# The low part of split weights: from a VectorE subtraction to a ScalarE pass and an accumulating DMA, in a one-core hybrid layer kernel

## The chip, the core and the metric

The kernel runs on one core of a Trainium2 chip. The core has a matrix engine (PE in the profile; its weight loads are listed as PEld), a vector engine (DVE), an activation engine (ACT), a general engine (POOL, GpSimd) and an engine that issues DMAs (SP). Each works through its own queue of instructions in order and waits on semaphores; DMAs run beside them on 16 DMA engines. The metric is the device time of one execution in microseconds; less is better. Before the change three runs took 1127.03, 1127.97 and 1128.79 us; the median is 1127.97 us.

## The reference

One layer for 512 prompt tokens and 64 sample tokens, each of width 1024. Three branches are fed by one projection of the normed input (`w_in`, 1024 rows), merged with sigmoid gates, and projected once more:

```python
h = _rmsnorm(x, norm_pre_w)
proj = h @ w_in
glu_v, glu_g, conv_gate, z, xbc, dt_raw, q, xa_gate, gates = jnp.split(proj, points, axis=-1)
u = glu_v * jax.nn.sigmoid(glu_g)                      # A: gated convolution, width 31
c, new_a = _causal_dwconv(u, st_a, conv_dw_w, conv_dw_b)
c = jax.nn.silu(_layernorm(c, conv_ln_w, conv_ln_b)) * jax.nn.silu(conv_gate)
out_a = c @ conv_out_w
...
y, new_h = _ssd_scan(xh, dt, a, bm, cm, st_h)          # B: state-space scan, 32 heads
...
out_b = y @ ssd_out_w
...
o = softmax(q k^T / 16) v                              # C: attention to 256 memory tokens, 4 heads
out_c = (o * jax.nn.silu(xa_gate)) @ xa_out_w
m = g[:, :, 0] * out_a + g[:, :, 1] * out_b + g[:, :, 2] * out_c
x_new = x + _rmsnorm(m @ w_out, norm_post_w)
```

The memory keys and values are computed for the prompt (`xa_kv_w`). Also returned are the keys and values, the tails of the two convolutions and the final states of the scan. All is in float32.

## The kernel before

The prompt and sample tokens are treated as one block of T = 576 columns. Activations lie with channels on the partitions, so a projection multiplies a weight tile of 128 columns with the normed input.

**Split arithmetic.** A float32 product is made of three matmuls in a rounded 32-bit type (float32r). Each operand is split in a high part, which is the value rounded to that type, and a low part, which is the rest. `mac` (L198 to L208) issues, for each block of 128 rows, high x high, high x low and low x high, so the low part of a weight (`wlo`) is first read by the third pair of matmuls of a job. `hT[0]` and `hT[1]` are the two parts of the normed input.

**Weight jobs.** `order` (from L89) is a list of 153 jobs in the order in which they are used: 512 KB of weights each, but for the narrow `dt`, for which 128 KB are loaded. `prep_to(n)` (L165 to L191) works this list up to job n: it takes a `raw`, a `whi` and a `wlo` tile from a pool with three buffers of each, loads `raw` through SP's queue (L172), makes the high part on ACT (L182) and the low part on DVE (L183):

```python
a = nc.scalar.activation(hi[:, :n_], raw[:, :n_], AF.Copy)
b = nc.vector.tensor_tensor(lo[:, :n_], raw[:, :n_], hi[:, :n_].bitcast(F32), ALU.subtract)
```

`W(name)` (L193) is called when a projection begins; it prepares the weights two jobs ahead (`LA = 2`). `dt` has lines of its own (L179, L180). With three buffers, the high part of a job can be written as soon as PE has done with the job three places before it, and PE reads it when the two jobs between are done.

**Stages.** After the start (norm and transposes of x, to about 25 us of the trace) comes the scan with four groups of heads, 20 chunks in all (`chunk_a`, `chunk_b`), whose small matmuls stand between projections for z, B, C and x and the output projection of the group before. Then follow the gated convolution's inputs (`glu`, with `gg` and `gv` jobs), the gates `g1`, the attention stage (four heads; jobs `k`, `q`, `v`, `xg`, where a `k` or `v` job has 24 matmuls of 256 columns, and any other but `dt` has 48 of about 288), the rest of the gates and output projections (`g2`, `oc`, `cg`, `g0`, `oa`), and the last projection, which loads and splits `w_out` at its own lines (L1075, L1083, L1084). The 31 taps of the long convolution (L768) run on DVE in the background of the attention and gate stages.

**What sets the order.** The program is written in a language whose scheduler simulates the engines and puts each engine's instructions in an order of its own, except where a line asks to keep the program's. So a change to some instructions can also move others. Semaphores are put in by it.

**Queues that the change touches.** SP issues the weight loads, each when its `raw` buffer is free, and, in the same queue, the scan's loads R (L497) and E (L516) of decay rows from a scratch tensor and the stores. POOL has 170 short instructions: copies of convolution tails (L445, L446), preparation of the padded inputs (L441, L442, L726, L727) and of the long convolution's tails (`utail`, L730, L731), and it issues no DMA.

Of the kernel before, what the change touches and what calls it, by code (L numbers as in the profile page):

```python
# [8 lines left out]
F32 = mybir.dt.float32  # L9
F32R = mybir.dt.float32r  # L10
AF = mybir.ActivationFunctionType
ALU = mybir.AluOpType
# [16 lines left out]
def hybrid_trunk_kernel(  # L29
# [9 lines left out]
    nc = tc.nc  # L39
# [15 lines left out]
    def ps_tile():  # L55
        return pps.tile([128, 512], F32, tag="ps", name="ps")

    # ------------------------------------------------------------ constants
    ident = const.tile([128, 128], F32, name="ident")
    make_identity(nc, ident)  # L60
    onesr = const.tile([128, 128], F32R, name="onesr")
# [14 lines left out]
    tails = const.tile([128, 2, 3, 24], F32, name="tails")  # L76
# [8 lines left out]
    msc = dram.tile([8, 128, T], F32, name="msc")  # L85
    scr = dram.tile([5, 32, 128], F32, name="scr")

    # ------------------------------------------------------------ weights
    order = []  # L89

    def wjob(name, src, c0, r0=0, kk=8, cols=128):
# [71 lines left out]
    nprep = [0]  # L163

    def prep_to(n):  # L165
        while nprep[0] <= min(n, len(order) - 1):
            name, src, c0, r0, kk, cols = order[nprep[0]]
            raw = wp.tile([128, 1024], F32, tag="raw", name="raw", bufs=3)
            hi = wp.tile([128, 1024], F32R, tag="whi", name="whi", bufs=3)
            lo = wp.tile([128, 1024], F32R, tag="wlo", name="wlo", bufs=3) if name != "dt" else hi  # L170
            n_ = kk * cols
            nc.sync.dma_start(  # L172
                out=raw[:, :n_].rearrange("p (k c) -> p k c", k=kk),
                in_=src[r0:r0 + 128 * kk, c0:c0 + cols].rearrange("(k p) c -> p k c", p=128),
            )
            if name == "dt":
                w = hi[:, :2 * n_].rearrange("p (k c) -> p k c", k=kk)
                rw, wh, wl = raw[:, :n_].rearrange("p (k c) -> p k c", k=kk), w[:, :, 0:32], w[:, :, 32:64]
                a = nc.scalar.activation(wh, rw, AF.Copy)  # L179
                b = nc.vector.tensor_tensor(wl, rw, wh.bitcast(F32), ALU.subtract)  # L180
            else:
                a = nc.scalar.activation(hi[:, :n_], raw[:, :n_], AF.Copy)  # L182
                b = nc.vector.tensor_tensor(lo[:, :n_], raw[:, :n_], hi[:, :n_].bitcast(F32), ALU.subtract)  # L183
            if nprep[0] in (2, 3):
                tc.keep_in_program_order(a)
                tc.keep_in_program_order(b)
            ready[name] = (w, None) if name == "dt" else (
                hi[:, :n_].rearrange("p (k c) -> p k c", k=kk),
                lo[:, :n_].rearrange("p (k c) -> p k c", k=kk),
            )  # L190
            nprep[0] += 1  # L191

    def W(name):  # L193
        i = pos[name]
        prep_to(i + LA)
        return ready.pop(name)
# [26 lines left out]
    def v2(ap):  # L223
        return ap.rearrange("p (a b) -> p a b", a=2)

    # ------------------------------------------------------------ start: x, parameters
    st = ExitStack()
    s2 = st.enter_context(tc.tile_pool(name="s2", bufs=2, reuse_waits="tile"))
    hl = [st.enter_context(tc.tile_pool(name="hl4", bufs=4, reuse_waits="tile"))]
# [8 lines left out]
        out=mask, in_=mask, pattern=[[1, 128]], compare_op=ALU.is_ge, fill=0.0,  # L238
# [4 lines left out]
    for t in range(5):  # L243
        n = 128 if t < 4 else 64
        if t < 4:
            x_t = obf[:, D * t:D * t + D]
        else:
            x_t = s2.tile([128, D], F32, tag="M", name="x4")
        nc.sync.dma_start(out=x_t[:n], in_=xp_d[128 * t:128 * t + 128] if t < 4 else xs_d)
        xt.append((x_t, n))  # L250
        if t == 0:
            wpre = s2.tile([128, D], F32, tag="R", name="wpre")
            nc.sync.dma_start(out=wpre, in_=norm_pre_w[0].partition_broadcast(128))
        if t == 1:
            prep_to(1)
# [58 lines left out]
    def tr_act(tiles, k, dst, wcol, ncols):  # L314
# [18 lines left out]
        out=after, in_=after, pattern=[[-1, 128]], compare_op=ALU.is_ge, fill=0.0,  # L333
# [64 lines left out]
        nc.scalar.activation(acsT[:, 512:640], pt[:32, 1, 0:128], AF.Copy)  # L398
        nc.sync.dma_start(out=scr.rearrange("c h l -> h c l"), in_=acsT.rearrange("p (c l) -> p c l", c=5))

    # parameters in channel-major columns
    vraw = s2.tile([104, 128], F32, tag="cbm", name="vraw")
    for o, src, n in (
        (V_PRE, norm_pre_w, 8), (V_MEM, mem_norm_w, 8), (V_GB, gate_b, 24), (V_DWB, conv_dw_b, 8),
# [28 lines left out]
            load_t(dww, 124 * i, flat(conv_dw_w, 124 * i, 124), 124, 0.5)  # L433
            load_t(sta, 120 * i, flat(state_conv_a[0], 120 * i, 120), 120, 2.0)

    # ------------------------------------------------------------ SSD
    def conv4(name, jt, tag, bufs, pt=None):
        if pt is None:
            pt = proj(name, HB)
        xp = s2.tile([128, 582], F32, tag="xp", name="xp")  # L440
        nc.gpsimd.memset(xp[:, 0:3], 0.0)  # L441
        nc.gpsimd.tensor_copy(xp[:, 515:518], sts.rearrange("p (r j) -> p r j", r=3)[:, :, jt])  # L442
        nc.scalar.activation(v2(xp[:, 3:515]), pt[:, :, 0:256], AF.Copy)
        nc.scalar.activation(xp[:, 518:582], pt[:, 1, 256:320], AF.Copy)
        nc.gpsimd.tensor_copy(tails[:, 0, :, jt], xp[:, 512:515])  # L445
        nc.gpsimd.tensor_copy(tails[:, 1, :, jt], xp[:, 579:582])  # L446
        acc = s2.tile([128, 579], F32, tag="acc", name="acc")
        w4 = scw.rearrange("p (r j) -> p r j", r=4)
        nc.scalar.activation(  # L449
            acc, xp[:, 0:579], AF.Identity, scale=w4[:, 0, jt:jt + 1], bias=half[:, V_SCB + jt:V_SCB + jt + 1]  # L450
        )
        for r in range(1, 4):
            nc.vector.scalar_tensor_tensor(acc, xp[:, r:r + 579], w4[:, r, jt:jt + 1], acc, ALU.mult, ALU.add)  # L453
        nc.scalar.activation(xp[:, 0:579], acc, AF.Tanh)
        o = sx.tile([128, 640], F32, tag=tag, name=tag, bufs=bufs)
        nc.gpsimd.memset(o[:, T:640], 0.0)
        nc.vector.scalar_tensor_tensor(o[:, 0:512], xp[:, 0:512], 1.0, acc[:, 0:512], ALU.add, ALU.mult)
        nc.vector.scalar_tensor_tensor(o[:, 512:576], xp[:, 515:579], 1.0, acc[:, 515:579], ALU.add, ALU.mult)
        return o
# [335 lines left out]
    glu(4, sx, "xs", 7)  # L795
    push_conv(2, 3)

    # tails of the short convolution
    for s, dst in ((0, o_csp), (1, o_css)):
        p = ps_tile()  # L800
        nc.tensor.transpose(p[:72, :128], tails[:, s].rearrange("p r j -> p (r j)"), ident)
# [2 lines left out]
        for r in range(3):  # L804
            nc.sync.dma_start(
                out=dst[0, 0, r].rearrange("(j c) -> j c", c=128), in_=tb[24 * r:24 * r + 24]
# [144 lines left out]
            if h != 2:  # L951
                push_conv(3 + h, 4 + h)

    # tails of the long convolution
    for b in range(2):
        p = ps_tile()
        for j in range(4):
# [4 lines left out]
        nc.sync.dma_start(out=o_cas[0, 0, :, 512 * b:512 * b + 512], in_=tu[30:60])  # L962
    st3.close()

    # ------------------------------------------------------------ out_c
    st3 = ExitStack()
    e2 = st3.enter_context(tc.tile_pool(name="e2", bufs=2, reuse_waits="tile"))
    hlA = st3.enter_context(tc.tile_pool(name="hlA", bufs=8, reuse_waits="tile"))
# [54 lines left out]
    stx.close()  # L1023
    stx = ExitStack()

    # ------------------------------------------------------------ layer norm, conv gate
    hlB = stx.enter_context(tc.tile_pool(name="hlB", bufs=8, side="right", reuse_waits="tile"))
    hl[0] = hlB
    chl, g0t = [], []
# [17 lines left out]
        merge(j, 0, g0t[j], f"oa{j}", cact2)  # L1047
        mhl.append(split(ob[:, j]))

    # ------------------------------------------------------------ output projection  # L1050
    npw = [
        e2.tile([128, NC], F32, tag="npw", name="npw0", bufs=1),
        c8.tile([128, NC], F32, tag="csum", name="npw1", bufs=1),
# [1 line left out]
    for q in range(2):  # L1055
        nc.sync.dma_start(
            out=npw[q][:, 0:512], in_=norm_post_w[0, 512 * q:512 * q + 512].partition_broadcast(128)
# [13 lines left out]
    for hf in range(2):  # L1071
        wo = []
        for k2 in range(4):
            raw = wp.tile([128, 1024], F32, tag="raw", name="raw", bufs=3)
            nc.sync.dma_start(  # L1075
                out=raw.rearrange("p (k c) -> p k c", k=2),
                in_=w_out[256 * k2:256 * k2 + 256, 512 * hf:512 * hf + 512].rearrange("(k p) c -> p k c", p=128),
            )
            for i in range(2):
                hi = hlB.tile([128, T], F32R, tag="hi", name="hi")  # L1080
                lo = hlB.tile([128, T], F32R, tag="lo", name="lo")
# [64 lines left out]
```

## Time and profile before

| | |
|---|---|
| median of 3 runs | 1127.97 us (1127.03 to 1128.79) |
| profiled execution, first to last instruction | 1125.1 us |
| L768, DVE, taps of the long convolution | x240, 191.7 us |
| L172, loads of 512 KB weights | x152, from `w_in` 104, `ssd_out_w` 16, `xa_kv_w` 16, `xa_out_w` 8, `conv_out_w` 8 |
| bytes moved by DMA | 122.06 MB, mean 108 GB/s |

The profiled execution's own time is known by its span: 1125.1 us from the first to the last instruction, 2.87 us under the median, which also holds what lies ahead of the first instruction and behind the last. In the rows of groups, a line of the program, its engine and operation, the tiles it writes and reads, their shape and the count are followed by busy time in us and the mean of one in ns, then the engine's idle time just before these instructions and what ended it. In the rows of a timeline, the start and the duration in us come first, and the idle time before stands in brackets. The clock in the windows is the share of full speed that PE was granted.

### The profile page before, as it was taken

To read this page: it belongs to the slowest core of one execution; us is meant where nothing else is said; L and a number is where in the kernel's file an instruction comes from. 1 tells how busy PE (TensorE), PEld (TensorE's weight loads), DVE (VectorE), ACT (ScalarE), POOL (GpSimd) and SP (SyncE) were. 2 spreads that over 40 slices of the span, in tenths; PEclk is the share of its full clock that TensorE was granted. 3 is DMA by queue.
4 is the path that set the end of the run, shared out by engine and by line. 5 is a ranking of instruction groups with operands and counts; after the bars stand their busy time and mean duration, and the time that the engine had idled before them with its cause. 6 is when DMAs were issued, how large, how long until landed. Compare 5 with 4: busy or idle time off the path is not lost.

```text
span 1125.1 us, 20180 instructions
## 1 busy us (share of the span) xinstructions
PE 1113.4 (99%) x8315; PEld 1077.6 (96%) x8315; DVE 834.8 (74%) x1269; ACT 487.7 (43%) x854; POOL 61.1 (5%) x170
## 2 busy tenths in 40 slices
PE   8999999999999999999999999999999999999997
PEld 7999999999999999999999999999999999999975
DVE  5778898588868796755999995997588869715534
ACT  5664664565537442543324343534512245422322
POOL 1100220021002100100000000000000000000000
PEclk9999999999999999999999999999999999999999
DMA  7354423432343232233444343434252233323412
GB/s 207 95 170 130 145 76 104 143 106 89 106 139 114 75 95 85 95 97 82 129 136 132 109 126 86 117 97 114 85 168 75 76 94 95 94 76 104 158 31 84
DMA packets 183586, 122.06 MB, mean 108 GB/s; under 512 B 6246, under 2 KB 173198, under 8 KB 183494
## 3 DMA queue, kind: packets, MB, share of 16 engines
q1 hardware_dynamic: 183494, 120.77, 36.5%
q8 instruction: 65, 1.06, 0.4%
q14 instruction: 27, 0.22, 0.1%
HBM read 111.44 MB, written 9.31 MB: 107 GB/s over the span
## 4 chain that ended last, share of the span: by engine, by line
PE 96%; DMA 2%; ACT 1%; DVE 0%; SPq 0%; issue 0%; DVEq 0%; ACTq 0%
PE mm L203 76%; PE ps L203 4%; PE ps L872 2%; PE ps L874 2%; PE ps L873 2%; PE ps L586 2%; PE ps L561 2%; PE ps L565 1%; DMA out_dram<-ho 1%; DMA ob<-in_x_prompt_dram 1%; PE ps L527 1%; PE ps L519 1%; DMA hin<-in_state_ssm_dram 1%; PE mm L345 0%; PE ps L483 0%; PE ps L846 0%
## 5 line engine op out<-in xcount | busy, mean ns | idle before, releaser
L203 PE MATMUL mm<-hT,whi 128*128 128x288 f32 (+2 forms) x3328 | 589.4, 297 | 0.6 <-DVE hT L279 0.3
L203 PEld LDWEIGHTS mm<-hT,whi 128*128 128x128 f32 x3328 | 495.2, 189 | 3.5 <-issue 1.5
L203 PE MATMUL mm<-hT,wlo 128*128 128x288 f32 (+2 forms) x1664 | 363.1, 297 | 0.0
L182 ACT ACTIVATE whi<-raw 128x1024 fp32r<-128x1024 f32 x152 | 160.9, 1059 | 421.6 <-PE mm L203 346.7
L203 PEld LDWEIGHTS mm<-hT,wlo 128*128 128x128 f32 x1664 | 273.8, 189 | 1.3 <-issue 1.1
L183 DVE TENSOR_TENSOR wlo<-raw,whi 128x1024 fp32r<-128x1024 f32 x152 | 185.8, 1222 | 117.6 <-ACT whi L182 117.1
L768 DVE SCALAR_TENSOR_TENSOR c<-u,dww,c 128x606 f32<-128x606 f32 x240 | 191.7, 845 | 0.0
L203 PE MATMUL mm<-hi,whi 128*128 128x288 f32 x512 | 111.4, 298 | 0.0
L203 PE MATMUL mm<-lo,whi 128*128 128x288 f32 x512 | 111.0, 297 | 0.0
L203 PE MATMUL mm<-hi,wlo 128*128 128x288 f32 x512 | 110.5, 296 | 0.0
L203 PEld LDWEIGHTS mm<-hi,whi 128*128 128x128 f32 x512 | 82.2, 188 | 0.9 <-issue 0.9
L203 PEld LDWEIGHTS mm<-lo,whi 128*128 128x128 f32 x512 | 82.5, 188 | 0.0
L203 PEld LDWEIGHTS mm<-hi,wlo 128*128 128x128 f32 x512 | 82.5, 188 | 0.0
L453 DVE SCALAR_TENSOR_TENSOR acc<-xp,scw,acc 128x579 f32<-128x579 f32 x72 | 58.4, 816 | 3.1 <-ACT acc L449 2.2
L203 PE MATMUL ps<-memT,whi 128*128 128x256 f32 x256 | 46.9, 283 | 0.0
L203 PEld LDWEIGHTS ps<-memT,whi 128*128 128x128 f32 x256 | 39.4, 189 | 0.0
L203 PE MATMUL ps<-memT,wlo 128*128 128x256 f32 x128 | 36.0, 281 | 0.0
L873 PE MATMUL ps<-lo,hi 128*128 128x512 f32 (+1 forms) x80 | 31.7, 396 | 0.0
L874 PE MATMUL ps<-hi,lo 128*128 128x512 f32 (+1 forms) x80 | 31.6, 395 | 0.0
L872 PE MATMUL ps<-hi 128*128 128x512 f32 (+1 forms) x80 | 30.8, 395 | 0.0
L547 ACT ACTIVATE M<-R,tok 128x128 f32<-128x128 f32 x80 | 25.5, 389 | 11.9 <-PE ps L586 11.9
L657 DVE TENSOR_TENSOR ob<-ob,mm 128x576 f32<-128x576 f32 x24 | 18.1, 752 | 15.1 <-PE mm L203 15.1
(280 smaller groups left out, 1243.4 us busy)
## 6 DMA issues: line engine op xcount, KB each, us to landing
raw<-in_w_in_dram SPq DMA_DIRECT2D x104, 512.0 KB
R<-scr SPq DMA_DIRECT2D x20, 512.0 KB
raw<-in_ssd_out_w_dram SPq DMA_DIRECT2D x16, 512.0 KB
raw<-in_xa_kv_w_dram SPq DMA_DIRECT2D x16, 512.0 KB
E<-scr SPq DMA_DIRECT2D x32, 128.0 KB
raw<-in_xa_out_w_dram SPq DMA_DIRECT2D x8, 512.0 KB
raw<-in_conv_out_w_dram SPq DMA_DIRECT2D x8, 512.0 KB
raw<-in_w_out_dram SPq DMA_DIRECT2D x8, 512.0 KB
```

The source lines that it names most:

```text
L182: a = nc.scalar.activation(hi[:, :n_], raw[:, :n_], AF.Copy)
L183: b = nc.vector.tensor_tensor(lo[:, :n_], raw[:, :n_], hi[:, :n_].bitcast(F32), ALU.subtract)
L203: m = nc.tensor.matmul(o, lhsT=w, rhs=r[:, s:s + w_], start=(i == 0 and a == 0), stop=(i == n - 1 and a == 2),)
L453: nc.vector.scalar_tensor_tensor(acc, xp[:, r:r + 579], w4[:, r, jt:jt + 1], acc, ALU.mult, ALU.add)
L547: nc.scalar.activation(M[:, 4 + e, :], R[:, 4 + e, :], AF.Relu, scale=-1.0, bias=tok[:, 0, c, a + 4:a + 5])
L561: nc.tensor.matmul(pS, lhsT=bt, rhs=xw, start=True, stop=True)
L586: nc.tensor.matmul(pd[o:o + 64, 128 * (e // 2):128 * (e // 2) + 128], lhsT=xd[:, 64 * e:64 * e + 64], rhs=M[:, e, :], start=True, stop=True,)
L657: nc.vector.tensor_tensor(v2(ob[:, m]), v2(ob[:, m]), va(pt), ALU.add)
L768: nc.vector.scalar_tensor_tensor(c, upad[j][:, r:r + NC], w31[:, r, j:j + 1], c, ALU.mult, ALU.add)
L872: nc.tensor.matmul(out, lhsT=wh, rhs=rh, start=(i == 0), stop=False)
L873: nc.tensor.matmul(out, lhsT=wh, rhs=rl, start=False, stop=False)
L874: nc.tensor.matmul(out, lhsT=wl, rhs=rh, start=False, stop=(i == n - 1))
```

## The change

For every weight job but the first six of the list, the low part is made in another way: ACT reads the raw tile a second time and writes its negative, rounded to float32r, into `wlo`; that is the negated high part. Then a DMA on POOL's queue adds the raw tile to `wlo`, which gives raw - high. The first six jobs (`B0`, `C0`, `dt` and the first three x) keep DVE's subtraction. The diff, without lines of comment that it takes out:

```diff
             else:
                 a = nc.scalar.activation(hi[:, :n_], raw[:, :n_], AF.Copy)
-                b = nc.vector.tensor_tensor(lo[:, :n_], raw[:, :n_], hi[:, :n_].bitcast(F32), ALU.subtract)
+                if nprep[0] < 6:
+                    b = nc.vector.tensor_tensor(lo[:, :n_], raw[:, :n_], hi[:, :n_].bitcast(F32), ALU.subtract)
+                else:
+                    nc.scalar.activation(lo[:, :n_], raw[:, :n_], AF.Copy, scale=-1.0)
+                    nc.gpsimd.dma_start(out=lo[:, :n_], in_=raw[:, :n_], accum_op=ALU.add)
             if nprep[0] in (2, 3):
                 tc.keep_in_program_order(a)
```

Lines behind this place have numbers higher by 4 in the changed kernel. A DMA from raw to `wlo` waits for the negated pass; PE's first matmul with `wlo`, and SP's next load into that `raw` buffer, wait for the DMA.

ACT's queue in the attention stage, at the start of the third head. Names are tiles with their buffer numbers: `whi` and `wlo` are parts of a weight, `kf` a projected key block, `c` the start of a long convolution. Before:

```order
L182 ACTIVATE whi_7908<-raw_7907 128x1024
L761 ACTIVATE c_7944<-u_7892,vecs_84,dww_86 128x606
L182 ACTIVATE whi_7948<-raw_7947 128x1024
L834 ACTIVATE kf_7938<-ps_7913 128x256
L836 ACTIVATE khi_7899<-kf_7938 128x256
L182 ACTIVATE whi_8011<-raw_8010 128x1024
L889 ACTIVATE qhi_7905<-mm_7953 128x576
```

The same place in the changed kernel:

```order
L182 ACTIVATE whi_7997<-raw_7996 128x1024
L186 ACTIVATE wlo_7998<-raw_7996 128x1024
L765 ACTIVATE c_8034<-u_7981,vecs_84,dww_86 128x606
L182 ACTIVATE whi_8038<-raw_8037 128x1024
L838 ACTIVATE kf_8028<-ps_8003 128x256
L186 ACTIVATE wlo_8039<-raw_8037 128x1024
L840 ACTIVATE khi_7988<-kf_8028 128x256
L182 ACTIVATE whi_8102<-raw_8101 128x1024
L893 ACTIVATE qhi_7994<-mm_8044 128x576
L186 ACTIVATE wlo_8103<-raw_8101 128x1024
```

Each high part is followed by the negated pass of the same raw tile, mostly behind one eviction of a matmul result (`kf`, `qhi`).

POOL's queue at that place and up to the next head, where `u` is the padded input of the long convolution and `utail` its tail. Before:

```order
L726 MEMSET u_7892 128x30
L727 COPY u_7892<-sta_87 128x30
L730 TENSOR_SCALAR utail_91<-u_7892 128x30
L731 TENSOR_SCALAR utail_91<-u_7892 128x30
L726 MEMSET u_8568 128x30
L727 COPY u_8568<-sta_87 128x30
```

The changed kernel:

```order
L730 MEMSET u_7981 128x30
L731 COPY u_7981<-sta_87 128x30
L187 DMA wlo_7927<-raw_7925 128x1024
L734 TENSOR_SCALAR utail_91<-u_7981 128x30
L735 TENSOR_SCALAR utail_91<-u_7981 128x30
L187 DMA wlo_7998<-raw_7996 128x1024
L187 DMA wlo_8039<-raw_8037 128x1024
L187 DMA wlo_8103<-raw_8101 128x1024
```

The accumulations stand between POOL's own instructions, and the one of `raw_7996` stands behind the two that wait for DVE's `u`.

## The prediction, made before the changed kernel was run

> **What bounds the kernel now.** I read the page's table of busy time first, then the windows by stage, then PE's waits.
>
> ```profile
> span 1125.1 us, 20180 instructions
> PE 1113.4 (99%) x8315; PEld 1077.6 (96%) x8315; DVE 834.8 (74%) x1269; ACT 487.7 (43%) x854; POOL 61.1 (5%) x170
> PEclk9999999999999999999999999999999999999999
> PE 96%; DMA 2%; ACT 1%; DVE 0%; SPq 0%; issue 0%; DVEq 0%; ACTq 0%
> 0.00:25.00 25.00, 20.74 (x153) 19.25 (x154) 15.41 (x24) 15.75 (x32) 3.34 (x30) 1.00 0.77 212
> 25.00:300.00 275.00, 274.21 (x2116) 263.42 (x2115) 218.48 (x380) 157.21 (x301) 31.47 (x89) 1.00 0.39 117
> 300.00:570.00 270.00, 269.88 (x2069) 263.19 (x2068) 204.82 (x314) 113.97 (x188) 20.36 (x39) 1.00 0.34 102
> 570.00:800.00 230.00, 230.00 (x1766) 227.01 (x1765) 196.42 (x285) 94.84 (x183) 4.28 (x10) 1.00 0.39 112
> 800.00:1050.00 250.00, 250.00 (x1886) 249.88 (x1885) 167.92 (x215) 84.70 (x107) 1.62 (x2) 1.00 0.35 101
> 1100.00:1125.10 25.10, 18.60 (x80) 13.39 (x78) 10.67 (x24) 4.87 (x14) 0.00 (x0) 0.92 0.27 94
> ```
>
> A row of windows gives its stretch, its length, and the busy time of PE, PEld, DVE, ACT and POOL, then the clock, the DMA share and GB/s. PE is idle for 4.26 us in the first 25 us, 6.50 us in the last 25, and 0.79 + 0.12 = 0.91 us between. The chain of waits is 96% PE. DVE at 74% is the second engine, but nothing on PE waits for it after the start. So the most that a lighter DVE can give back in the middle is 0.9 us; the head uses the six weight jobs that the change leaves alone, and the tail splits its weights at other lines.
>
> **What the change removes and adds.**
>
> ```profile
> L182 ACT ACTIVATE whi<-raw 128x1024 fp32r<-128x1024 f32 x152 | 160.9, 1059 | 421.6 <-PE mm L203 346.7
> L183 DVE TENSOR_TENSOR wlo<-raw,whi 128x1024 fp32r<-128x1024 f32 x152 | 185.8, 1222 | 117.6 <-ACT whi L182 117.1
> ```
>
> There are 152 such jobs; five of the first six (the sixth is the narrow `dt`) keep the subtraction. DVE loses 147 x 1.222 = 179.6 us, from 834.8 to about 655. ACT gains 147 passes of the same size as L182: 147 x 1.059 = 155.7 us, to about 643, 57% of the span. Both are off the path: 0 us each as busy time. What counts is when `wlo` is ready.
>
> The time that is to be had I read from two stretches, the dense one near the end and the attention stage, where half the jobs (`k`, `v`) are half as long.
>
> ```profile
> 985.64 1.06 ACT L182 ACTIVATE whi<-raw 128x1024 fp32r<-128x1024 f32 x1 [4.71 <-issue]
> 986.61 0.73 ACT L715 ACTIVATE lo<-mm,half 128x576 f32<-128x576 f32 x1
> 986.74 1.23 DVE L183 TENSOR_TENSOR wlo<-raw,whi 128x1024 fp32r<-128x1024 f32 x1 [5.17 <-ACT whi L182]
> 999.00 0.42 PE L203 MATMUL mm<-hT,wlo 128*128 128x288 f32 x2
> ...
> 588.42 1.06 ACT L182 ACTIVATE whi<-raw 128x1024 fp32r<-128x1024 f32 x1 [6.47 <-PE ps L203]
> 593.66 0.43 PE L203 MATMUL mm<-hT,wlo 128*128 128x288 f32 x2
> ...
> 686.32 1.06 ACT L182 ACTIVATE whi<-raw 128x1024 fp32r<-128x1024 f32 x1 [7.71 <-PE mm L203]
> 687.57 0.90 ACT L761 ACTIVATE c<-u,vecs,dww 128x606 f32<-128x606 f32 x1 [0.19 <-DVE u L729]
> 689.36 1.06 ACT L182 ACTIVATE whi<-raw 128x1024 fp32r<-128x1024 f32 x1 [0.89 <-PE ps L203]
> 690.32 0.37 ACT L834 ACTIVATE kf<-ps 128x256 f32<-128x256 f32 x1
> 695.85 0.28 PE L203 MATMUL ps<-memT,wlo 128*128 128x256 f32 x1
> 698.99 0.29 PE L203 MATMUL mm<-hT,wlo 128*128 128x288 f32 x1
> ```
>
> In each pair ACT starts the high part as soon as PE has released the buffer of three jobs earlier, and PE's first `wlo` matmul of that job follows 13.36 us later in the dense stretch (985.64 to 999.00), and 9.53 us (686.32 to 695.85) or 9.63 us (689.36 to 698.99) in the attention stage. The tightest in the trace is 5.24 us (588.42 to 593.66). Now DVE needs 2.3 us of that. After the change: high part 1.06, in most jobs one eviction of a finished matmul between (0.73 dense, 0.37 attention), negated pass 1.06, then the accumulating DMA. It may take 13.36 - 2.85 = 10.5 us in the dense stretch and 9.63 - 2.49 = 7.1 us in the attention stage before PE waits. The order of the changed kernel gives 101 matmuls or more between release and reader in the dense stretch, as before, and 66 to 91 for 19 attention jobs; the two shortest, 66 and 67, are at the 9.53 us per 77 of the row above some 8.2 us, which leaves 5.5 us for the DMA. The job at 688 gets one more delay: its DMA stands on POOL behind L734 and L735, which wait for the `u` that DVE ended at about 687.5:
>
> ```profile
> L730 POOL TENSOR_SCALAR utail<-u 128x30 f32<-128x30 f32 x8 | 7.2, 904 | 306.8 <-DVE u L728 306.8
> L731 POOL TENSOR_SCALAR utail<-u 128x30 f32<-128x30 f32 x8 | 4.6, 572 | 0.0
> ```
>
> That is issue at 687.5 + 0.90 + 0.57 = 689.0 and 6.8 us to its reader, much like the others. These waits, 306.8 us in all, now have DMAs queued behind them; the lighter DVE can only shorten them.
>
> **The unknown: how long the DMA takes.** The trace has no DMA from POOL, none inside SBUF and none that adds. The nearest rows are a 512 KB load that its reader was waiting for, and what it moved:
>
> ```profile
> 1087.86 0.37 SPq L1075 DMA_DIRECT2D raw<-in_w_out_dram  x1
> 1091.55 1.16 ACT L1083 ACTIVATE hi<-raw 128x512 fp32r<-128x512 f32 x2 [0.16 <-DMA raw<-in_w_out_dram]
> 1088.88:1091.19 2.31, 2.31 (x12) 1.54 (x11) 1.73 (x3) 1.43 (x3) 0.00 (x0) 1.00 0.77 225
> q1 hardware_dynamic: 183494, 120.77, 36.5%
> ```
>
> From issue to use 3.69 us, of which 2.31 moving at 225 GB/s. Below: the addition costs nothing and it takes 3.7 us. Above: three passes (raw, old value, result) one after another, and one raw load ahead of it, 3.7 + 3 x 2.3 = 10.6 us. I take two reads for each write, 3.7 + 2.3 = 6.0 us, nearest to the row. At the DMA share of 0.77 in that window, moving then costs 147 x 4.6 x 0.77 = 521 us of all 16 engines, 46% of the span beside the 36.5% of now: 83% in all, so accumulations and loads will meet, and the upper part of the bounds is real.
>
> The Trainium skill (DMA: Bandwidth & Descriptors, "Anatomy of one DMA — SWDGE (gpsimd) path") puts a GpSimd-issued DMA at about 2.0 us plus bytes over 436 GB/s; by that page an estimate of 3.2 us here, and no job would be late. No run here shows such a DMA yet; its fit is for plain copies.
>
> **SP's queue.** The load of the next raw tile now waits for the accumulation instead of DVE.
>
> ```profile
> SPq L172 <- DVE wlo L183: 616.6, 116, 14.6
> 987.99 0.37 SPq L172 DMA_DIRECT2D raw<-in_conv_out_w_dram  x1
> 1004.80 1.06 ACT L182 ACTIVATE whi<-raw 128x1024 fp32r<-128x1024 f32 x1 [4.71 <-PE mm L203]
> ACT E L517 <- DMA E<-scr: 17.9, 12, 2.1
> ```
>
> The load issued at 987.99 is used at 1004.80, 16.8 us later, and needs 3.7. The buffer is released later by 2.85 + 6.0 - 2.3 = 6.5 us, which leaves 6.6 us: nothing. Behind the waiting load on SP stand R and E of the scan, for which ACT already waits 17.9 us; PE is covered there by the projections that fill the scan.
>
> **The sum.** 1125.1 us of span, plus two attention jobs late by 6.0 - 5.5 = 0.5 us each, plus 0 elsewhere: 1126.1. The median of 1127.97 is 2.87 us over the profiled span, so 1129.0 us, no change within 0.2% (2.3 us, about what a measurement of this kernel can tell).
>
> **Rivals.**
> 1. *The DMA takes 7 to 10.5 us.* PE then waits in the attention stage. A stall gives the next two jobs the same time, for there are three buffers; of the 19 tight jobs about nine pay, two of them 1.6 us more. At 8.5 us: 7 x 1.4 + 2 x 3.0 = 16 us, 1144; at 10.4: 7 x 3.3 + 2 x 4.9 = 33 us, 1161. It decides from 7.1 us on. For it: DMA share 0.39 in this stage already. Against it: 6.0 as the nearest sum. Chance 0.20.
> 2. *POOL is kept from issuing by DVE*, busy 196.4 of 230 us in the attention stage. If every accumulation waits there for DVE's instructions in progress, some three 0.85 us taps of L768 (191.7 us over 240 in the page's groups below), 6.0 becomes 8.5 and the price is again 16 us, 1144. The trace has no POOL issue that shows it. Chance 0.05. The Trainium skill (SBUF — State Buffer, "SBUF: two separate sides") says that a VectorE instruction in a 2-port mode locks GpSimd out and starves its DMAs of descriptors, about 620 ns becoming about 3100; the same page excludes instructions with two tensor inputs such as these taps, which is why I give it little.
>
> ```profile
> L768 DVE SCALAR_TENSOR_TENSOR c<-u,dww,c 128x606 f32<-128x606 f32 x240 | 191.7, 845 | 0.0
> ```
>
> 3. *The DMA takes over 10.5 us.* Then every chain of three jobs in the dense stretches, some 33, pays the excess: at 12 us 33 x 1.5 + 45 of the attention stage = 95 us, 1223. Chance 0.12.
> 4. *SP's head blocks R and E*, the scan's 20 chunks come late, and PE waits: if one in four loses 3 us, 15 us, 1143. Against it: E mostly waits for its own buffer. Chance 0.07.
> 5. *Faster.* Only a better order of the scan could do that, by PE's own time, since waits give 0.9 us. By over 2.3 us: 0.04, say 1125.
>
> **How the numbers follow.** My forecast has 0.52. Faster 0.04, same 0.52, slower 0.20 + 0.05 + 0.12 + 0.07 = 0.44. The forecast's own range is 1127 to 1130. The range for 8 in 10 starts at 1126.8 and goes to 1152, past the middle of rivals 1, 2 and 4; it leaves out rival 3 and the top of rival 1.
>
> **What would show it.** L183 left with 5 instructions, the negated pass with 147 of about 1.06 us; DVE near 655 us, ACT near 643; PE still 1113 us with under 3 us of waits between 25 and 1100, none on a DMA except in the attention stage; the span of an accumulation from issue to first reader. A PE wait of several us on `wlo` DMAs at every third job in 800 to 1050 would show rival 3, one in 570 to 800 alone rivals 1 or 2, waits of scan matmuls in 60 to 420 rival 4. A negated pass that is later than its PE release by more than 3 us, or a raw tile that lands after its buffer is free, would break the step on ACT or SP.

## The result, and the profile after

The changed kernel takes 1158.0 us (median of 4 runs, 1155.98 to 1159.46), the kernel before, on the same chip, 1128.01 us (4 runs). The ratio is 1.0262, with a 95% interval of 1.0247 to 1.0278: slower by 30.0 us, and outside the predicted range. The page of the changed kernel, its totals and the chain of waits:

```profile
span 1154.3 us, 20522 instructions
...
PE 1123.4 (97%) x8315; PEld 1085.5 (94%) x8315; DVE 674.1 (58%) x1122; ACT 624.6 (54%) x1003; POOL 166.8 (14%) x317
...
DMA  7487767667675766567889998989698777768712
...
PE 85%; DMA 9%; ACT 3%; DVE 2%; issue 1%; SPq 1%; DVEq 0%; ACTq 0%; POOLq 0%
```

The span grew by 29.2 us. PE does the same 8315 matmuls; its busy time is 10.0 us more (1123.4 against 1113.4), and its idle time 19.2 us more (30.9 against 11.7). So there are two losses to find: waits, and matmuls that run longer. The windows by stage say where:

```profile
25.00:300.00 275.00, 265.56 (x2020) 254.81 (x2019) 177.51 (x334) 182.34 (x324) 47.59 (x118) 0.99 0.71 171
300.00:570.00 270.00, 259.57 (x1962) 251.19 (x1961) 150.36 (x263) 142.21 (x226) 41.29 (x75) 0.97 0.68 161
570.00:800.00 230.00, 229.29 (x1761) 226.64 (x1760) 166.48 (x254) 124.61 (x200) 36.61 (x48) 1.00 0.89 201
800.00:1050.00 250.00, 250.00 (x1881) 249.20 (x1879) 123.39 (x181) 128.12 (x169) 34.48 (x43) 1.00 0.78 177
```

PE is idle 9.4 and 10.4 us in the first two windows, where it was idle 0.8 and 0.1 before (they hold the scan and, behind it, the convolution's inputs and the gates `g1`), and of the four these alone have a clock below 1.00. The attention stage, which I had watched, loses 0.7 us, and the dense stretch nothing, although the DMA engines are busier there (0.89 and 0.78) than in the first two windows (0.71 and 0.68). The waits of PE after the start name what was late:

```profile
PE ps L513 <- DMA hin<-in_state_ssm_dram: 7.3, 3, 4.9
PE ps L322 <- DVE mt L265: 4.7, 1, 4.7
PE mm L207 <- ACT ob L659: 2.5, 1, 2.5
PE mm L398 <- ACT tok L393: 2.1, 1, 2.1
PE ps L420 <- DMA praw<-in_conv_dw_w_dram: 1.6, 1, 1.6
...
PE mm L207 <- DVE sz L468: 1.5, 1, 1.5
...
PE mm L207 <- DMA wlo<-raw: 0.6, 1, 0.6
```

A row gives what waited and for what, the total in us, the number of waits and the longest. Only the last is a low part that came late. `hin` (a group's old state, 256 KB, L508) and `praw` (64 KB at most, L418) are loads on SP's queue that PE itself transposes. `mt` (the memory tokens, two loads of 512 KB, L795) stands in the same queue and reaches PE through ACT and DVE: ACT waited 6.5 us for it, and PE 4.7 us for DVE. `ob` stood on ACT behind the `E` of the scan, for whose load ACT waited 4.0 us. `tok` and `sz` stood on ACT and DVE, behind no late load. So the waits that hang on a late load of SP's queue are 7.3 + 4.7 + 2.5 + 1.6 = 16.1 us. The clock at the waits, and behind two that are a little shorter, in windows of the changed kernel:

```profile
64.90:68.20 3.30, 3.27 (x15) 3.01 (x16) 2.98 (x6) 1.85 (x5) 0.60 (x3) 0.50 1.11 247
127.00:130.40 3.40, 3.40 (x28) 3.40 (x29) 3.37 (x6) 2.66 (x5) 0.15 (x1) 1.00 0.63 118
173.40:176.80 3.40, 3.40 (x25) 3.40 (x26) 3.40 (x7) 2.43 (x3) 0.61 (x4) 1.00 0.44 105
228.70:232.00 3.30, 3.30 (x15) 3.30 (x15) 0.00 (x0) 3.23 (x5) 0.00 (x0) 0.50 1.02 317
348.20:354.90 6.70, 4.35 (x20) 4.35 (x21) 2.55 (x5) 1.09 (x3) 0.00 (x0) 0.50 0.54 135
508.60:515.30 6.70, 4.52 (x19) 4.36 (x20) 3.94 (x8) 4.41 (x8) 1.01 (x1) 0.50 0.26 60
```

Behind the waits of 2.1 (`tok`) and 2.5 us (`ob`) the clock is 0.50 over windows of 3.3 us. At the waits of 4.9 (`hin`, 345.7 to 350.6 us) and 4.7 us (`mt`, 506.0 to 510.8) it is 0.50 over 6.7 us, which begin in the last 2.4 us of the wait. Behind `hin` at 127 and `sz` at 173, 1.7 and 1.5 us, it stays at 1.00. In the four windows at half speed PE is busy for 3.27 + 3.30 + 4.35 + 4.52 = 15.4 us; at half speed that is work of 7.7 us, so the clock accounts for 7.7 of the 10.0 us that PE's busy time grew by. Of the rest, 1.4 us is there without any such window too (run 13 below).

The DMA queues and the accumulations, with the size of one in KB and the median time from issue to landing in us:

```profile
q0 software_dynamic: 21168, 77.08, 36.4%
q1 hardware_dynamic: 183494, 120.77, 36.4%
...
wlo<-raw POOLq DMA_DIRECT2D x147, 512.0 KB, 5.5
```

The accumulations move 77 MB and take as much of the 16 DMA engines as all loads and stores (q1), which move 121 MB.

### The profile page after: what moved, and what is told of

The parts are those of the page before. It is cut to its first block, busy times and chain, and to the rows that moved or that the text cites. A ratio compares the mean times of both kernels' runs of the same rounds, so it can differ in the third digit from the quotient of the medians.

```text
span 1154.3 us, 20522 instructions
## 1 busy us (share of the span) xinstructions
PE 1123.4 (97%) x8315; PEld 1085.5 (94%) x8315; DVE 674.1 (58%) x1122; ACT 624.6 (54%) x1003; POOL 166.8 (14%) x317
## 3 DMA queue, kind: packets, MB, share of 16 engines
q0 software_dynamic: 21168, 77.08, 36.4%
q1 hardware_dynamic: 183494, 120.77, 36.4%
## 4 chain that ended last, share of the span: by engine, by line
PE 85%; DMA 9%; ACT 3%; DVE 2%; issue 1%; SPq 1%; DVEq 0%; ACTq 0%; POOLq 0%
PE mm L207 67%; PE ps L207 3%; PE ps L876 2%; PE ps L877 2%; PE ps L878 2%; DMA E<-scr 2%; DMA wlo<-raw 2%; PE ps L565 1%; DMA out_dram<-ho 1%; PE ps L590 1%; DMA hin<-in_state_ssm_dram 1%; PE ps L569 1%; DMA ob<-in_x_prompt_dram 1%; DMA mt<-in_mem_prompt_dram 1%; PE ps L531 1%
## 5 line engine op out<-in xcount | busy, mean ns | idle before, releaser
L187 POOL DMA_DIRECT2D wlo<-raw x147 | 126.7, 862 | 700.3 <-ACT wlo L186 585.2
L772 DVE SCALAR_TENSOR_TENSOR c<-u,dww,c 128x606 f32<-128x606 f32 x240 | 187.9, 845 | 2.2 <-ACT c L765 2.2
L186 ACT ACTIVATE wlo<-raw 128x1024 fp32r<-128x1024 f32 x147 | 154.3, 1050 | 0.0
L984 DVE SCALAR_TENSOR_TENSOR lo<-lo,mm 128x576 f32<-128x576 f32 x8 | 6.0, 755 | 67.3 <-PE mm L207 67.3
```

What stands on the lines that cost most here:

```text
L186: nc.scalar.activation(lo[:, :n_], raw[:, :n_], AF.Copy, scale=-1.0)
L187: nc.gpsimd.dma_start(out=lo[:, :n_], in_=raw[:, :n_], accum_op=ALU.add)
L772: nc.vector.scalar_tensor_tensor(c, upad[j][:, r:r + NC], w31[:, r, j:j + 1], c, ALU.mult, ALU.add)
```

## The experiments

Each difference is against the median of the kernel before, run beside it on the same chip. "Same order" below means that the rows of every engine's queue stand in the same order in two kernels; otherwise the scheduler moved some.

**1. The negated pass without the DMA.**

```diff
-                    nc.gpsimd.dma_start(out=lo[:, :n_], in_=raw[:, :n_], accum_op=ALU.add)
+                    b = nc.vector.tensor_tensor(lo[:, :n_], raw[:, :n_], lo[:, :n_].bitcast(F32), ALU.add)
```

> As the changed kernel, but DVE adds the raw tile to the negated high part, where the DMA did (same result). So ACT has its second pass, DVE its old work, POOL no DMA. Theory A (the DMA is the cause: raw loads wait for it at SP's head, and its bytes slow the small loads behind them): PE's waits on hin, mt, praw and E go, and what is left is the wait of PE on ACT's tok (2.1 us, plus some 1.7 us for the 3.41 us at half clock behind it): 1128 to 1132 us. Rival B (ACT's second pass, or the other order of instructions that comes with it, is the cause): most of the 30 us stay, 1145 us or more. Rival C (DVE relieved is what changed the order): 1128 us.

1131.65 us, ratio 1.0036 (1.0023 to 1.0049): 4.2 us over before. The second pass on ACT, with the order that the scheduler made of it, costs something, and not much. PE's new waits in this run:

```profile
PE mm L398 <- ACT tok L393: 1.4, 1, 1.4
PE ps L389 <- DVE dtw L381: 1.2, 1, 1.2
```

Rival B falls as the main cause; its 4 us are real.

**2. Accumulations from the attention stage on.** `if nprep[0] < 6` becomes `if nprep[0] < 76`. The first 76 jobs are those of the scan, of the convolution's inputs made before the attention, of `g1`, and one `k`; the first accumulation starts at 576.6 us.

> As the changed kernel, but DVE keeps the subtraction for the first 76 jobs, that is for the whole scan; the DMA adds for the 77 jobs behind it (same result). The windows of the changed kernel put its whole loss between 25 and 570 us. Theory A (the loss is made in the scan, by small loads behind raw loads on SP): within 2 us of before, 1127 to 1130 us, although half of all accumulations remain. Rival D (every accumulation costs its share, by contention or by later low parts, wherever it stands): half of the 30 us, about 1143 us.

1139.05 us, ratio 1.0101 (1.0086 to 1.0116): 11.6 us over before. Neither expectation is right. The scan has hardly any loss now (no wait there is over 0.5 us), but now PE waits 6.1 us for low parts in the attention stage, where the changed kernel waited 0.6. PE's waits in this run:

```profile
PE mm L207 <- DMA wlo<-raw: 5.4, 3, 2.0
...
PE ps L207 <- DMA wlo<-raw: 0.7, 1, 0.7
```

**3. The DMA nearly without bytes.**

```diff
-                    nc.gpsimd.dma_start(out=lo[:, :n_], in_=raw[:, :n_], accum_op=ALU.add)
+                    nc.gpsimd.dma_start(out=lo[:, 0:64], in_=raw[:, 0:64], accum_op=ALU.add)
```

> As the changed kernel, but the DMA adds columns 0 to 63 of 1024 alone; the addition for the other columns is left out. The count of DMAs, POOL's issues and every wait stay; the bytes of the DMA go to a sixteenth. Theory A1 (what counts is that SP's head waits for a DMA, however short): the raw load still leaves later by the negated pass and the fixed part of a DMA, some 1.1 + 2 to 3 us instead of 6.5; the waits on hin and mt shrink but stay, 1133 to 1145 us. Theory A2 (what counts is the bytes: 77 MB that share the 16 DMA engines with the loads): hin, E and mt land as before, 1128 to 1133 us with the wait on ACT's tok left.

1131.97 us, ratio 1.0036 (1.0023 to 1.0049), 4.5 us over before, as without any DMA. That is 0.3 us from run 1, less than the intervals can tell apart (the orders differ): 147 accumulating DMAs, their issues on POOL (861 ns each, as in the changed kernel) and the waits for them cost nothing that shows. The rest comes with the bytes, either by their own traffic or because they hold `raw` longer.

**4. Raw loads on ACT's queue.** In L172, `nc.sync` becomes `nc.sync if nprep[0] < 6 else nc.scalar`.

> As the changed kernel, but from the seventh job on the raw loads are issued by ACT's queue, not SP's (same result, same bytes). SP then has the small loads and the stores alone, so nothing of the scan stands behind a waiting raw load on SP; ACT's own work now stands behind the waiting raw loads. Theory A1 (the head of SP's queue): PE's waits on hin, praw and mt shrink to under 2 us each; if ACT's queue isn't blocked in its place, 1128 to 1138 us; if it is, waits of PE on ACT take their place and the time is above 1158 us. Theory A2 (the bytes): hin and mt still land 5 to 8 us after issue, and the time stays at 1145 to 1158 us.

1233.53 us, ratio 1.0930 (1.0912 to 1.0949). ACT's queue is blocked in the place of SP's (PE now waits 14.8 us for `xs` of L719 on ACT), as the second branch of the expectation has it. One thing can be read from PE's waits: with no raw load on SP behind the sixth job, PE still waits for `hin`.

```profile
PE ps L513 <- DMA hin<-in_state_ssm_dram: 8.3, 3, 5.1
```

**5. A hold by short DMAs that read raw.** The kernel before, and behind its subtraction:

```diff
+                if nprep[0] >= 6:
+                    nc.gpsimd.dma_start(out=jk, in_=raw[:, 0:8])
+                    nc.gpsimd.dma_start(out=jk, in_=raw[:, 8:16])
```

> The kernel before, with DVE's subtraction, and from the seventh job on two DMAs on POOL's queue, one behind the other, that read eight columns each of the raw tile into a tile that nothing reads (result unchanged). They hold the raw buffer for two short DMAs, which at the 2.2 us of the DMA of the run with 64 columns is some 4.4 us longer than before, about what the accumulation holds it, and move nearly no bytes. Theory A1 (SP's head held by late raw buffers): PE waits on hin, mt or praw, and 1133 to 1150 us. Theory A2 (bytes): PE has no new wait, 1127 to 1130 us.

1134.05 us, ratio 1.0064 (1.0041 to 1.0087). This was a poor test of the hold: the short DMAs start when `raw` lands, not when DVE is done, so only 25 raw loads waited for them (74.8 us), and DVE still released the other 114. What it lost is elsewhere, in POOL's timeline:

```profile
63.70 0.54 POOL L186 DMA_DIRECT2D jk<-raw  x1 [0.90 <-DMA jk<-raw]
64.27 0.12 POOL L380 MEMSET tok<- 64x32 f32 x1
```

A memset of 0.12 us that DVE's `dtw` needs stood on POOL behind DMAs that waited for one another, and PE waited 3.0 us for `dtw`. It says nothing on theory A1.

**6. The bytes without the hold.** The kernel before, and behind its subtraction two plain copies per job to a scratch tensor:

```diff
+                if nprep[0] >= 6:
+                    for r_ in range(2):
+                        nc.gpsimd.dma_start(out=jd[2 * (nprep[0] % 2) + r_], in_=hi[:, :n_].bitcast(F32))
```

> The kernel before, with DVE's subtraction, and from the seventh job on two plain DMAs of 512 KB on POOL's queue per job, from whi to a scratch tensor that nothing reads (result unchanged). The raw buffer isn't held by them; whi is, until they have read it. They load the 16 DMA engines about as the accumulations do (DMA digits 6 to 9 on the page). Theory A2 (bytes): hin, E and mt land 5 to 8 us after issue as in the changed kernel, PE waits on them, 1140 us or more. Theory A1 (SP's head): raw loads leave as before, 1127 to 1131 us. If PE waits on whi instead, the run tells neither.

1140.72 us, ratio 1.0110 (1.0092 to 1.0127): 13.3 us over before.

```profile
q0 software_dynamic: 42336, 154.16, 39.6%
```

That is the queue of the copies on the page. The waits of SP's queue and of PE:

```profile
SPq L173 <- DVE wlo L184: 627.1, 119, 14.2
...
PE ps L513 <- DMA hin<-in_state_ssm_dram: 5.6, 2, 3.3
```

Raw loads wait for DVE as before (627.1 us against 616.6), but PE waits 5.6 us on `hin`. So traffic without a hold of `raw`, at about the share that the accumulations take, costs some 13 us; the copies go to a tensor outside SBUF, and the order is another.

**7. Half of the columns.** The DMA adds `lo[:, 0:512]` and `raw[:, 0:512]` alone.

> As the changed kernel, but the DMA adds columns 0 to 511 of 1024 alone; the addition for the others is left out. With 64 columns the time was 1132.0 us, with all 1158.0. If the price goes with the bytes: half of the 26 us, 1145 us. If it starts where hin, mt and praw use up the time they have (a threshold, as my account of waits has it): under 1137 us, and no PE wait over 2.1 us but the one on tok.

1140.94 us, ratio 1.0122 (1.0107 to 1.0137): 13.6 us, between 4.5 and 30.0 and somewhat nearer to the first. The longest wait is the 2.1 us on `tok`, but `hin` (4.1 us in three) and `praw` (1.8) are there too. No threshold shows between 64 and 512 columns; the order is not that of the changed kernel.

**8. Accumulations up to the attention stage alone.** `if nprep[0] < 6` becomes `if nprep[0] < 6 or nprep[0] >= 76`.

> As the changed kernel, but the DMA adds for jobs 7 to 76 alone, the scan's; from job 77 on DVE subtracts (same result). The other half, accumulations behind the scan alone, cost 11.6 us. If the two halves add up: 30.5 - 11.6 = 19 us, 1146 us. If the scan has the whole loss of the changed kernel, as its windows show it, and the attention stage pays only where the scan hasn't made PE late: 1156 to 1158 us.

1153.89 us (1152.03 to 1159.26), ratio 1.0242 (1.0216 to 1.0268): 26.5 us over before, most of the 30.0, and some 2 us under the second of the two expectations. With 11.6 us of run 2 the halves would make 38.1 us, so they don't add up.

**9. The hold without bytes, mended.** The kernel before, and behind its subtraction:

```diff
+                if nprep[0] >= 6:
+                    nc.gpsimd.dma_start(out=raw[:, 0:8], in_=lo[:, 0:8].bitcast(F32))
+                    nc.gpsimd.dma_start(out=raw[:, 0:8], in_=lo[:, 8:16].bitcast(F32))
```

> The kernel before, with DVE's subtraction, and from the seventh job on two DMAs on POOL's queue, one behind the other, that overwrite eight columns of the raw tile with columns of wlo once DVE has made it (nothing reads raw then; result unchanged). Two of 1.9 us, with POOL's issues, hold the raw buffer some 5 us beyond DVE's subtraction, as long as the accumulation does, and move nearly no bytes; this is the hold that the earlier run with reads of raw alone gave only for 25 of its loads. Theory A1 (SP's head held by late raw buffers is enough): PE waits on hin, mt, praw, and 1137 us or more. Theory A2 (bytes are needed): 1127 to 1131 us.

1126.76 us, ratio 0.9989 (0.9980 to 0.9998). SP's queue now waits for these DMAs before nearly every raw load, about as long as for the plain copies of run 13 (665.7 us; the changed kernel has 758.7):

```profile
SPq L173 <- DMA raw<-wlo: 696.0, 133, 9.8
```

PE has no new wait. A held buffer, and a head of SP's queue that stands 696 us, cost nothing in this run, where the loads behind it are fast. Theory A1 by itself falls.

**10. Hold and bytes, without the addition and without the negated pass.** In the place of run 9's two DMAs:

```diff
+                    nc.gpsimd.dma_start(out=raw[:, :n_], in_=lo[:, :n_].bitcast(F32))
```

> The kernel before, with DVE's subtraction, and from the seventh job on one plain DMA of 512 KB on POOL's queue that copies wlo over raw inside SBUF (nothing reads raw then; result unchanged). So the raw buffer is held by a DMA of the accumulation's bytes, PE doesn't wait for that DMA, and ACT has no second pass. Theory A (hold and bytes together make the loss): most of the 30.5 us less the 4.2 us of the negated pass, 1148 to 1155 us, with the waits on hin, mt and praw. Theory A2 (bytes alone): about what the plain copies to a scratch tensor cost, 1138 to 1142 us. If the addition itself is what makes the accumulation long, the copy lands in under 4 us and the time stays below 1140 us.

1131.93 us, ratio 1.0037 (1.0023 to 1.0052), 3.7 us over before. The last sentence of the expectation is what came, by the page's rows of the queue and of the DMA:

```profile
q0 software_dynamic: 21168, 77.08, 18.1%
...
raw<-wlo POOLq DMA_DIRECT2D x147, 512.0 KB, 3.5
```

Same packets, same bytes as in the changed kernel, half the time on the DMA engines, and 3.5 us to landing. Theory A as I had put it, any DMA of these bytes, falls too. The addition is the candidate that is left; this run differs from the changed kernel in more than that, and runs 12 and 13 test it alone.

**11. The small loads on ACT's queue.** In the changed kernel, the DMAs of `ho` (L490), `hin` (L508), `praw` (L418) and `mt` (L795) are issued by `nc.scalar`.

> As the changed kernel, but the stores ho and the loads hin, praw and mt are issued by ACT's queue, not behind the raw loads on SP (same result). Theory A1 (they are late because they stand behind waiting raw loads): their waits, 14 us of PE's 20 in the changed kernel, shrink by most, and with the half clock behind them the time falls to 1138 to 1146 us. Theory A2 (they are late because their bytes move slowly beside the accumulations): hin and mt still need 5 to 8 us from issue to landing, and the time stays at 1150 us or more.

1144.20 us, ratio 1.0154 (1.0136 to 1.0173), 16.0 us over before: 14 of the 30.0 come back. PE's waits on `hin` fall from 7.3 to 2.3 us, on `praw` to 1.1, on `mt` to none over 0.2:

```profile
PE mm L207 <- DMA wlo<-raw: 3.1, 2, 2.5
...
PE ps L513 <- DMA hin<-in_state_ssm_dram: 2.3, 3, 1.1
```

So with accumulations of full length the place behind the raw loads does matter (the scheduler moved other rows too, so not all of the 14 need be due to the place). What the run does not give back are `ob` behind `E` (2.7 us), the negated pass before `tok` (2.1), and low parts that are now late in the attention stage.

**12. The addition without the negated pass.** Run 10 with the addition as its only difference; the order is the same:

```diff
-                    nc.gpsimd.dma_start(out=raw[:, :n_], in_=lo[:, :n_].bitcast(F32))
+                    nc.gpsimd.dma_start(out=raw[:, :n_], in_=lo[:, :n_].bitcast(F32), accum_op=ALU.add)
```

> The kernel before, with DVE's subtraction, and from the seventh job on one accumulating DMA of 512 KB on POOL's queue that adds wlo to raw (nothing reads raw then; result unchanged). It is the run with the plain copy over raw, 1131.9 us, with the addition as its one difference: same bytes, same hold, no negated pass, and PE doesn't wait for it. Theory A (the addition's own time on the 16 DMA engines, with the hold, makes the scan's small loads late): DMA engines near 73% as in the changed kernel, waits on hin, mt and praw, and 1146 to 1156 us. Rival B2 (the negated pass and its order are needed too): under 1138 us.

1145.78 us, ratio 1.0160 (1.0146 to 1.0173): 18.3 us over before, 14.6 more than the plain copy.

The DMA queue is that of the changed kernel (36.4%):

```profile
q0 software_dynamic: 21168, 77.08, 36.5%
```

PE's waits, with line numbers lower by one:

```profile
PE ps L512 <- DMA hin<-in_state_ssm_dram: 9.5, 4, 4.1
PE ps L589 <- DVE M L555: 2.9, 1, 2.9
```

No matmul waits for this DMA, and ACT has no extra pass: the low parts and their readers are those of before. It is a hair under the lower end of what theory A gave, and 8 us over rival B2's. There is no wait on `mt` here, which theory A also named.

**13. The changed kernel without the addition**, in the changed kernel's own order:

```diff
-                    nc.gpsimd.dma_start(out=lo[:, :n_], in_=raw[:, :n_], accum_op=ALU.add)
+                    nc.gpsimd.dma_start(out=lo[:, :n_], in_=raw[:, :n_].bitcast(F32R))
```

> As the changed kernel, but the DMA copies the raw tile over wlo and adds nothing, so the low part is wrong by the high part: the addition is left out. Instructions, bytes and waits are those of the changed kernel. Theory A (the addition's own time on the DMA engines): 3.5 us to landing and 18% for that queue, and the price of the plain copy and of the negated pass alone, 3.8 + 4.2 us: 1133 to 1138 us. Rival B2 (the negated pass, its order and the waits make the loss together with any DMA of these bytes): 1145 us or more.

1132.48 us, ratio 1.0051 (1.0037 to 1.0065): 5.0 us over before, half a us under what theory A gave and far from rival B2's. Instructions, bytes, order, and what waits for what are those of the changed kernel; the addition alone makes 30.0 - 5.0 = 25.0 us. PE is idle 3.8 and 0.6 us in the windows 25 to 300 and 300 to 570, at a clock of 1.00, and its busy time is 1114.8 us. Its waits on `hin`, `ob` and `praw` are gone; what is left after the start:

```profile
PE mm L398 <- ACT tok L393: 2.1, 1, 2.1
...
PE mm L207 <- DVE sz L468: 1.5, 1, 1.5
...
PE ps L322 <- DVE mt L265: 0.4, 1, 0.4
```

So the waits for `tok` and `sz` are there without the addition, and the 16.1 us that hang on SP's loads shrink to 0.4. The same two rows of the page:

```profile
q0 software_dynamic: 21168, 77.08, 19.8%
...
wlo<-raw POOLq DMA_DIRECT2D x147, 512.0 KB, 3.2
```

One place can be laid side by side, since the order is the same. The timeline of SP's queue before the third group's `hin`, and behind it PE's transposes of it, first without the addition:

```profile
325.22 1.48 SPq L520 DMA_DIRECT2D E<-scr  x2
328.41 0.38 SPq L172 DMA_DIRECT2D raw<-in_w_in_dram  x1
328.89 0.52 SPq L490 DMA_DIRECT2D out_dram<-ho  x1
...
333.27 0.38 SPq L508 DMA_DIRECT2D hin<-in_state_ssm_dram  x1
```

```profile
336.49 0.66 PE L513 MATMUL ps<-ident,hin 128*128 128x128 f32 x4
```

and in the changed kernel:

```profile
334.24 1.24 SPq L520 DMA_DIRECT2D E<-scr  x2
340.23 0.37 SPq L172 DMA_DIRECT2D raw<-in_w_in_dram  x1
340.71 1.78 SPq L490 DMA_DIRECT2D out_dram<-ho  x1
...
345.38 0.38 SPq L508 DMA_DIRECT2D hin<-in_state_ssm_dram  x1
```

```profile
350.55 1.12 PE L513 MATMUL ps<-ident,hin 128*128 128x128 f32 x4 [4.89 <-DMA hin<-in_state_ssm_dram]
```

From the issue of `E` to the transposes it is 11.3 us without and 16.3 us with the addition: 5.0 us, PE's wait of 4.9. Of these, 2.8 us lie before the raw load, which waits for its accumulation (6.0 us behind `E` against 3.2), 0.3 us between raw load and `hin`, which waits for the store of `ho` in its buffer, and 2.0 us in the load of `hin` itself (5.2 us from issue to use against 3.2). So more than half of this wait is SP's head, the rest a slower transfer.

## Why the prediction was wrong, point by point

**What bounds the kernel** was right: with PE at 99%, nothing could be gained, and DVE's lower load (the rows that make low parts fell from 185.8 to 6.1 us) brought nothing.

**DVE and ACT.** The negated pass has 147 instructions of 1.05 us, 154.3 us against my 155.7. That it is off the path, "0 us each as busy time", was wrong by some 4 us: run 1, with the pass and no DMA, loses 4.2 (its other order included), and in the changed kernel PE waits 2.1 us for `tok`, which stood on ACT behind such a pass. I had asked only when `wlo` is ready, not what stands behind the new pass on ACT.

**The time from issue to landing** was well sized: 6.0 us forecast, 5.5 measured; the 3.2 us that stood beside it is what the plain copy of run 13 took. **The budget of the low parts** held as well: 0.6 us of waits for them in the changed kernel against the sum's 1.0. (By the prediction's own figures the two shortest jobs leave 8.2 - 2.49 = 5.7 us, not 5.5, so that term should have been 0.6; this changes nothing else.) Run 2, where the attention stage did lose 6.1 us by the same DMAs, shows how little was left: rival 1's mechanism, though its point of 7.1 us lay above the median of 5.7 measured there (the longest took 10.3). Why the changed kernel was spared there isn't settled; the orders differ. Rival 2 did not show: POOL's issues of the accumulations took 842 to 1014 ns each, so DVE did not keep POOL from issuing them.

**SP's queue is the step that failed.** It was put at nothing: a raw load had 6.6 us left, R and E stand behind the waiting load, and "PE is covered there by the projections that fill the scan". Three errors are in it. The load that I checked, at 987.99 us, lies in the dense stretch, which lost nothing; the loss lies before 570 us. I counted R and E, but not `hin`, `mt`, `praw` and the store of `ho`, which stand in the same queue and whose readers are transposes on PE or lead to them. And I kept a load's 3.7 us from the trace without accumulations. I had even worked out that 83% of the DMA engines' time would be asked for, and that accumulations and loads would meet, but I brought that only to the accumulation's own landing, not to every other load beside it. In the place of 0 us the runs show 25.0 us for the addition: PE's waits on SP's loads, 16.1 us against 0.4 without it, and the half clock at them. The later release of `raw` by itself is not it: run 9 has 696 us of waiting at SP's head and loses nothing. Rival 4 had most of the place (waits of scan matmuls between 60 and 420 us; the one for `mt` comes at 506), at 0.07 and 15 us; its size was half, and its mechanism was short of the bytes.

**What the sum lacked** is the clock. No term of mine had PE slower after a wait; the trace shows 7.7 of the 29.2 us there. The longer idle time is 19.2 us, not far from rival 4's 15.

**The addition** is the cause that the runs single out: 25.0 us in the changed kernel's order, 14.6 in the other. An accumulation takes 36.4% x 16 x 1154.3 / 147 = 45.7 us of one DMA engine's time, a plain copy of the same packets 19.8% x 16 x 1130.0 / 147 = 24.4 us. I had estimated 147 x 4.6 x 0.77, or 46%; the size was near, its effect wasn't drawn. The Trainium skill (Collectives: The Full Stack, "The bandwidth ceiling: the fold count and why AG ≠ RS ≠ AR") says of the ring collectives that a reduction in the DMA path reads two sources for each write, and so gives about half the rate of a copy; by its rule 2 x 24.4 = 48.8 us would be expected here, an estimate, and the 45.7 us agree within 7%. The longer issue on POOL (862 ns against 530) is not the cause: run 3's DMAs have it too.

The parts don't add up: negated pass and plain copy 5.0 us, negated pass without a DMA 4.2, accumulation without the pass 18.3, all together 30.0. That late loads and a fuller ACT queue meet in the same stretch, where a wait can bring a stretch of half clock with it, would fit this; no run shows it apart from the different orders. How the 25 us divide over the queue's head and slower transfers I can show for the one `hin` above and by run 11's 14 us, not for every wait.

## What to carry to other kernels

When a job is moved from an engine to a DMA, work out what it takes of the DMA engines' time, and then go through every other transfer of that stage, the rare small ones first, and ask which of them a matmul reads directly; a mean over the stage hides them. An accumulating DMA counted nearly twice here (45.7 us against 24.4). And price a wait of the bounding engine at more than its length where the trace shows that its clock falls at it.

## What the runs showed of the hardware

- An accumulating DMA of 512 KB inside SBUF, from POOL's queue, landed 5.5 us after issue (median), a plain one 3.2 us in the same order of instructions; POOL needed 862 ns to issue the first and 530 ns for the second. The DMA's own line in the changed kernel, with the shortest, median and longest issue in ns:

```profile
L187 POOL DMA_DIRECT2D wlo<-raw x147: 842/862/1014, 44.6 to 1074.3; - x147
```

  and in run 13:

```profile
L187 POOL DMA_DIRECT2D wlo<-raw x147: 527/530/997, 44.6 to 1050.0; - x147
```

- PE's granted clock fell to 0.50 at waits that were shorter than I would have thought, in the changed kernel from 2.1 us on, for about 3.4 or 6.8 us. The Trainium skill (TensorE: Matmul & The Clock Gate, "Part 1: The HAM clock gate (the "warmup" mystery)") has the clock drop after an idle window of about 3.4 us, and the window running freely; the length of the dips agrees with that window, the waits of 2.1 and 2.5 us that were followed by one are shorter than it. After the same wait of 2.1 us for `tok` (62.9 to 65.0 us) run 13 had no dip, by the window behind it:

```profile
65.00:68.40 3.40, 3.40 (x27) 3.35 (x28) 3.08 (x6) 1.65 (x5) 0.23 (x2) 1.00 0.56 178
```

  So the length of a wait alone doesn't decide it. In run 12 the wait of 2.9 us for `M` (81.7 to 84.5 us) had no dip behind it, the clock is 1.00 up to 88.0; in run 7 the wait of 1.8 us for `praw` had one, from 270.7 to 274.1 us.
